# The opening of an encoder block: sums as 128 equal columns, and a new order of loads, rows and scalings

## The chip, the cores and the metric

The kernel runs on one core of one Trainium2 chip. The metric is the time of one execution on the device in microseconds (us), less is better. The core has five engines that run beside each other: PE (TensorE, matrix products), DVE (VectorE), ACT (ScalarE), POOL (GpSimd) and SP (SyncE, which here only issues transfers), and DMA engines that move data between the chip's memory (DRAM), and the on-chip memory (SBUF). PE writes into a second on-chip memory, PSUM.

## The reference

One encoder layer over 1024 positions of width 1024, in float32, conditioned by a vector c:

```python
ada = silu(c) @ w_ada + b_ada                 # 6 x 1024 numbers
shift1, scale1, gate1, shift2, scale2, gate2 = split(ada, 6)
h = rmsnorm(x, g_mix) * (1 + scale1) + shift1
qa, ka, va, qb, kb, vb, ga, gb = split(h @ w_in)
# dilated attention on a, 2-D neighbourhood attention on b, gated merge, w_out
x = x + gate1 * (merged @ w_out)
# second norm with shift2, scale2; w_up, depthwise conv, gelu gate, w_down; final rmsnorm
```

What matters here is the beginning: before the first product of `h` with `w_in` can run, the kernel needs the norm of x (a sum of squares over the 1024 features of every position) and the numbers shift1 and scale1, which come from a product of the vector silu(c) with the 1024 x 2048 first columns of `w_ada`.

## The kernel before, in words

**Layout.** x is kept transposed, features on the 128 partitions, in eight tiles `x[0][k]` of 128 x 512 (the first half of the positions) and eight `x[1][k]` (the second half). A feature product is a sum over k = 0 to 7. Every operand of a product is split in two, a high part rounded to PE's reading format and a low part, the rest, and a product is three: high x high, high x low, low x high. ACT makes the high parts (L57, L229), DVE or POOL the low ones (L61, L231).

**w_ada.** It comes in ten pieces of 512 columns. The first four pieces are shift1 and scale1, cut so that piece q holds what the two feature tiles k = 2q and 2q+1 need: a quarter. A piece is eight rows `wt[q][t]` of 128 x 512. The sum over t and over the partitions is made in two ways. `ada_rows` (L169) lets DVE multiply a row by `cs[:, t]`, a number per partition, and add it to a 128 x 512 sum (`acc`, which lies in PSUM under the name pv); `ada_sums` (L153) lets PE sum over the partitions: four products with a 128 x 128 block of the row as weights and one column moving, which gives one column of four in PSUM (`pada`). Its column is `cs[:, t]` for a row that DVE left alone and `ones` for what DVE added up. `add_sums` (L95) does the same for the squares of x (`pcol`). `piece_bias(q)` (L290) adds b_ada (L293) and makes the scale `am1` (L295). `scaled` (L225) then lets ACT compute h from x with that scale and bias, high part (L229) and the whole once more (L230), and gives DVE's low part (L231) to be called later.

**The opening, in one written order.** Lines 419 to 612 stand in a block in which the program order is the order of every engine's queue: SP, ACT, DVE, POOL and PE each take their instructions one after the other, as they are written. SP's loads are: x[0] (four pairs), the small vectors, piece 0, the first half (k = 0 to 3) of two q/k weight tiles (`half_load(qk_raw, ...)`), the first half of two v weight tiles (`v_raw`), piece 1, the second halves, piece 2, piece 3 row by row, x[1], two more v weight tiles (`v_raw1`) and then pairs of rows of pieces 4 to 9 (`pair_load`). Meanwhile PE runs `warm` (L233), products of ones that are never read. Then come:

- the squares of x[0] (ACT L450, DVE L452), their sum over partitions on PE (L454), the norm's factor r on DVE and ACT (L458 to 461), its spread to all partitions by four transposes (`bcast`, L108, called at L463), and in between PE's sums of rows 0, 1 and 2 of piece 0 and DVE's rows 3 to 7, which PE sums at L474;
- x[0][0] and x[0][1] times the spread factor `pb` (L473); `pbs` is a copy of `pb` in SBUF (L470);
- the loop over q (L476): `piece_bias`, x[0][2] and x[0][3] times `pb` on DVE and x[0][4] to x[0][7] times `pbs` on POOL (both in q = 0), `scaled` for two k, the splits of v weights (`v_split`) and of the second half of q/k weights (`qk_split(1)`, q = 1), DVE's rows of the next piece in portions around the low parts (`steps`), the first rows of the piece after that (L499), and on PE the products of q and k (`qk_products`, L305), the sums of the next piece, and the products of v (`v_parts`, L312).

**After it.** From L518 on the block does v for the second half of the v columns, the norm and modulation of x[1] (`modulate`, L212), and a loop over `v_steps` (L578): in each step PE makes v for one or two blocks of 128 positions (`v_wide`), DVE adds rows of pieces 4 to 9 (`row_pairs`, up to `row_ends[n]`), ACT copies v out of PSUM and SP stores it (`v_out`, L284, through the tile `vs` with two buffers). At L553 and L551 stand the row sums, at L600 and L605 the last sums of each piece. After the block the rest of v (`v_steps[9:]`, L629) and the attention follow.

Of the kernel before, what the change touches and what calls it, by code (L numbers as in the profile page):

```python
# [19 lines left out]
KT = 8  # L20
# [9 lines left out]
def hybrid_encoder(tc, xT, c, w_ada, small, w_in, p1_bias, p23_bias, na_bias, ln2_mult, ident, w_br, w_out,  # L30
# [62 lines left out]
    qkpool = tc.alloc_tile_pool(name="qk", bufs=4)  # L93

# [189 lines left out]
    def v_out(br, st, p, c0=0):  # L284
        vs = work.tile([128, 512], FT, name="vs", bufs=2)[:, :p.shape[-1]]
        act.activation(vs, p, AF.Copy)
        sp.dma_start((va_s, vb_c)[br][st * 128:st * 128 + 128, c0:c0 + p.shape[-1]], vs)
# [17 lines left out]
    def qk_products(ks):  # L305
        for k in ks:
            mhi, mlo = h[0, k]
            for x_, (part, m) in enumerate(((0, mhi), (1, mhi), (0, mlo))):
                for p, w in zip(qk_psum, qk_w):
                    pe.matmul(p, w[part][:, k], m, start=k + x_ == 0, stop=k == KT - 1 and x_ == 2)  # L310
# [108 lines left out]
    with tc.manual_schedule(engines={e.engine for e in (sp, act, dve, pool, pe)}):  # L419
# [26 lines left out]
        warm(35, idle, True)  # L446
# [6 lines left out]
        pcol = ps_n.tile([128, KT], FT, name="pcol")  # L453
# [4 lines left out]
        dve.tensor_scalar(r, pcol[:, :4], 1.0 / D, EPS, OP.mult, OP.add)  # L458
        act.activation(r, r, AF.Sqrt)
        ada_rows(wt[0], acc, range(3, 4), 3, 7)  # L460
# [3 lines left out]
        warm(3, idle, True)  # L464
        ada_sums([(wt[0][1], cs[:, 1:2])], pa, stop=False)
        warm(4, idle, True)
        ada_sums([(wt[0][2], cs[:, 2:3])], pa, stop=False)
        warm(2, idle, True)
        pbs = early.tile([128, 512], FT, name="mt", bufs=3)
        act.activation(pbs, pb, AF.Copy)  # L470
        ada_rows(wt[0], acc, range(4, 8), 3, 7)
        for k in range(2):
            dve.tensor_tensor(x[0][k], x[0][k], pb, OP.mult)  # L473
        ada_sums([(wt[0][7], ones)], pa)  # L474
        warm(5, idle, True)
        for q in range(4):  # L476
            ks = range(2 * q, 2 * q + 2)
            piece_bias(q, pa)
            if q == 0:
                for k in range(2, 4):  # L480
                    dve.tensor_tensor(x[0][k], x[0][k], pb, OP.mult)
                stage = [ps_n.tile([128, 512], FT, name=n) for n in ("pcol", "pbc")]
            low = [scaled(x[0][k], k) for k in ks]
            if q == 0:
                v_split(v_raw, (pool, pool), slice(0, 4), v_w[0])
                for k in range(4, 8):
                    pool.tensor_tensor(x[0][k], x[0][k], pbs, OP.mult)
# [12 lines left out]
            if q == 2:  # L500
                accs = sq_accs()
                square(x[1], accs, range(4), dve)
            if q == 3:
                v_split(v_raw1, (dve, pool), slice(0, KT), v_w[1])
                square(x[1], accs, range(4, 8), dve)
            qk_products(ks)
            if q == 0:
                pa = ada_sums([(wt[1][t], cs[:, t:t + 1]) for t in (6, 7)], stop=False)
                v_parts(0, range(4), ks, (0,))
                ada_sums([(wt[1][5], ones)], pa)  # L510
                v_parts(0, range(4), ks, (1, 2))
                continue
            v_parts(0, (0,), ks, range(3))
# [26 lines left out]
        row_ends = (4, 7, 10, 12, 14, 17, 19, 22, 24)  # L540
# [37 lines left out]
        for n, step in enumerate(v_steps[:9]):  # L578
# [50 lines left out]
    for br, st in v_steps[9:]:  # L629
        v_out(br, st, *v_wide(st))  # L630
# [1279 lines left out]
```

## Time and profile before

| | us |
|---|---|
| median of 3 runs | 1500.61 |
| lowest and highest of them | 1496.16, 1501.8 |
| the profiled execution, its own time | 1498.67 |
| span of its trace | 1496.8 |
| PE busy in the span | 1474.4 |
| DVE, ACT, POOL busy | 939.0, 773.6, 760.6 |

The span is the time from the first to the last instruction in the trace; the time of an execution has 1.87 us more around it. In rows of the trace the first number is the start in us from the span's start, the second the duration (where it says x3, the stretch of three), then engine, line and operation, then what is written <- what is read, with shapes, and in brackets how long the engine stood idle before and what ended that. PEld are PE's weight loads, which run beside its products. A product in plain float32 appears as two records, so a sum of four products is eight. POOL's durations are rough. In tables of stretches the columns are: stretch, its length, busy time and number of records of PE, PEld, DVE, ACT and POOL, the clock granted to PE (1.00 is full), the mean busy share of the DMA engines, and GB/s.

### The profile page before, as it was taken

Reading aid. Unit: us, or ns where it says so; the run is one execution under the profiler, and the core shown is the slowest. Engines: PE = TensorE matmul, PEld = TensorE weight load, DVE = VectorE, ACT = ScalarE, POOL = GpSimd, SP = SyncE. Lnnn points to the kernel's source line nnn. Section 1 sums busy time; section 2 is a strip of 40 time slices with the busy share of each in tenths; the row PEclk is TensorE's granted clock in tenths of the full one; section 3 lists DMA queues with packets and bytes.
Section 4 is the critical chain, followed back from the end, with each engine's and each line's share of the span. In section 5 each row is a group of like instructions: output and inputs, shape, how many; then the busy total and the mean of one; then the engine's idle time right before and its main releaser. Section 6 shows DMA issues by size and latency. Waiting matters only on the chain.

```text
span 1496.8 us, 21659 instructions
## 1 busy us (share of the span) xinstructions
PE 1474.4 (98%) x7664; PEld 1251.9 (84%) x7664; DVE 939.0 (63%) x1763; ACT 773.6 (52%) x1442; POOL 760.6 (51%) x633
## 2 busy tenths in 40 slices
PE   9999999999999999999999999999999999999997
PEld 8888888889798998888888778888888888877887
DVE  7683446465555665556515897666666667886865
ACT  4531666666655666653345464444444447474542
POOL 3031332434234454512268668766666776978811
PEclk9999999999999999999999999999999999999999
DMA  9577332444645555577544313222222233542313
GB/s 371 183 277 268 88 99 68 143 114 129 170 144 145 144 160 166 172 243 260 194 153 143 104 43 141 85 85 85 85 83 84 71 136 116 197 148 64 104 41 113
DMA packets 117301, 210.29 MB, mean 140 GB/s; under 512 B 42788, under 2 KB 55716, under 8 KB 117156
## 3 DMA queue, kind: packets, MB, share of 16 engines
q1 hardware_dynamic: 116632, 208.57, 43.4%
q8 instruction: 60, 0.98, 0.3%
q14 instruction: 49, 0.40, 0.1%
q10 hardware_dynamic: 560, 0.33, 0.1%
HBM read 163.58 MB, written 42.66 MB: 138 GB/s over the span
## 4 chain that ended last, share of the span: by engine, by line
PE 81%; DVE 5%; POOL 5%; DMA 4%; issue 2%; ACT 2%; SPq 0%; DVEq 0%; POOLq 0%; ACTq 0%
PE pj L84 10%; PE pj L86 10%; PE pj L85 10%; PE pj L1308 10%; PE pj L1307 10%; PE pj L1306 10%; PE pj L402 3%; PE O L1013 2%; DMA wraw<-w_down 2%; PE T L1000 1%; PE S L978 1%; POOL wsl L61 1%; PE pv L279 1%; PE pv L281 1%; PE pv L280 1%
## 5 line engine op out<-in xcount | busy, mean ns | idle before, releaser
L61 POOL TENSOR_TENSOR wlo<-wraw,whi 128x512 fp32r<-128x512 f32 (+1 forms) x84 | 106.1, 1284 | 144.8 <-ACT whi L57 129.8
L84 PE MATMUL pj<-h,whi 128*128 128x512 f32 x432 | 178.1, 412 | 0.4 <-DVE kl L374 0.4
L86 PE MATMUL pj<-h,wlo 128*128 128x512 f32 x432 | 169.8, 393 | 0.0
L85 PE MATMUL pj<-h,whi 128*128 128x512 f32 x432 | 169.4, 392 | 0.0
L1306 PE MATMUL pj<-op,wsh 128*128 128x512 f32 x408 | 159.1, 391 | 3.7 <-ACT wsh L57 2.7
L1307 PE MATMUL pj<-op,wsh 128*128 128x512 f32 x408 | 159.1, 390 | 0.9 <-DVE op L1237 0.6
L1308 PE MATMUL pj<-op,wsl 128*128 128x512 f32 x408 | 157.8, 390 | 0.7 <-POOL wsl L61 0.7
L667 DVE TENSOR_TENSOR tl<-T,th 128x512 fp32r<-128x512 f32 (+3 forms) x120 | 77.2, 654 | 101.2 <-ACT th L666 99.9
L717 POOL TENSOR_TENSOR wlo<-wraw,whi 128x512 fp32r<-128x512 f32 x58 | 74.4, 1293 | 126.8 <-ACT whi L716 126.7
L61 POOL TENSOR_TENSOR wsl<-big,wsh 128x512 fp32r<-128x512 f32 (+1 forms) x86 | 111.7, 1320 | 42.5 <-ACT wsh L57 37.6
L659 ACT ACTIVATE P<-P,st 128x256 f32<-128x256 f32 x128 | 64.2, 503 | 93.9 <-DVE st L658 93.9
L1543 DVE SCALAR_TENSOR_TENSOR big<-pj,sm,big 128x512 f32<-128x512 f32 (+2 forms) x183 | 94.9, 563 | 16.5 <-ACT big L1537 15.6
L86 PEld LDWEIGHTS pj<-h,wlo 128*128 128x128 f32 x432 | 81.1, 188 | 18.0
L1306 PEld LDWEIGHTS pj<-op,wsh 128*128 128x128 f32 x408 | 76.6, 188 | 21.9 <-ACT wsh L57 4.0
L1307 PEld LDWEIGHTS pj<-op,wsh 128*128 128x128 f32 x408 | 76.6, 188 | 18.2 <-DVE op L1237 1.2
L1308 PEld LDWEIGHTS pj<-op,wsl 128*128 128x128 f32 x408 | 76.6, 188 | 17.4 <-POOL wsl L61 1.8
L84 PEld LDWEIGHTS pj<-h,whi 128*128 128x128 f32 x432 | 81.5, 189 | 11.5 <-issue 0.8
L1308 PE MATMUL pj<-op,wlo 128*128 128x512 f32 x232 | 90.3, 389 | 0.0
L1307 PE MATMUL pj<-op,whi 128*128 128x512 f32 x232 | 90.3, 389 | 0.0
L1306 PE MATMUL pj<-op,whi 128*128 128x512 f32 x232 | 90.3, 390 | 0.0
L85 PEld LDWEIGHTS pj<-h,whi 128*128 128x128 f32 x432 | 81.7, 189 | 10.1
L61 POOL TENSOR_TENSOR wsl<-wraw,wsh 128x384 fp32r<-128x384 f32 (+1 forms) x46 | 57.3, 1268 | 62.1 <-ACT wsh L57 54.5
(398 smaller groups left out, 4173.6 us busy)
## 6 DMA issues: line engine op xcount, KB each, us to landing
wraw<-w_in SPq DMA_DIRECT2D x32, 512.0 KB
wada<-w_ada SPq DMA_DIRECT2D x31, 512.0 KB
big<-w_up SPq DMA_DIRECT2D x22, 512.0 KB
wraw<-w_up SPq DMA_DIRECT2D x22, 512.0 KB
big<-as SPq DMA_DIRECT2D x22, 512.0 KB
as<-big SPq DMA_DIRECT2D x21, 512.0 KB
gs<-gs SPq DMA_DIRECT2D x32, 256.0 KB
g<-gs SPq DMA_DIRECT2D x16, 512.0 KB
```

What stands on the lines that cost most here:

```text
L61: lo_eng.tensor_tensor(lo[:, i:i + step], raw[:, i:i + step], f(hi)[:, i:i + step], OP.subtract)
L84: pe.matmul(psum, whi[:, k0 + k], mhi, start=k == 0, stop=False)
L85: pe.matmul(psum, whi[:, k0 + k], mlo, start=False, stop=False)
L86: pe.matmul(psum, wlo[:, k0 + k], mhi, start=False, stop=k == n - 1)
L402: pe.matmul(p[:, 256 * r:256 * r + 256], ww[:, k], m[:, r], start=k + x + r == 0, stop=k == KT - 1 and x == 2, skip_group_check=True)
L659: act.activation(pp, pp, AF.Exp, bias=mi, scale=-1.0, accum_out=li)
L667: dve.tensor_tensor(tl[:m, :n], pt[:m, :n], f(th)[:m, :n], OP.subtract)
L717: pool.tensor_tensor(lo[:, i:i + n], raw[:, i:i + n], f(hi)[:, i:i + n], OP.subtract)
L1306: pe.matmul(psum, whi[:, k], bhi, start=j < 4 and k == 0, stop=False, skip_group_check=True)
L1307: pe.matmul(psum, whi[:, k], blo, start=False, stop=False, skip_group_check=True)
L1308: pe.matmul(psum, wlo[:, k], bhi, start=False, stop=k == n - 1, skip_group_check=True)
L1543: dve.scalar_tensor_tensor(y[:, dst], src, wt, y[:, dst], OP.mult, OP.add)
```

## The change

It has six parts.

1. `wide_sums` takes the place of `ada_sums` and `add_sums` in the opening: the moving operand is the column repeated 128 times, so each of the four products gives 128 equal columns, 512 in all. `every` picks column 0 of each 128. It is used for the squares of x[0], for the sums of piece 0, and for the sums of piece 1; later ones stay as they were.
2. Of the 52 dummy products 42 are left: 38 ahead of the sum of squares (35 before) and 4 ahead of the loop.
3. The order around the norm: DVE's row 3 of piece 0 comes ahead of the norm's factor, row 4 between its parts, rows 5 to 7 behind; on PE the sums of rows 0 and 1 come ahead of the transposes.
4. Loads: piece 1 is loaded ahead of the first half of v_raw, and piece 2 ahead of the second halves of the q/k and v weights.
5. In q = 0 POOL scales x[0][2] to x[0][7], DVE none of them; row 3 of piece 1 goes from DVE to PE, between the products of k = 0; one row of piece 3 goes from the end of q = 1 to the first portion of q = 2.
6. In the loop over `v_steps` the stores of v are issued by ACT in place of SP, and a tenth step is in the loop.

```diff
+    def wide_sums(dst, blocks, col, first=False):
+        for m in range(4):
+            cc = slice(m * 128, m * 128 + 128)
+            pe.matmul(dst[:, cc], blocks[:, cc], col.to_broadcast([128, 128]), start=first and m == 0, stop=False,
+                      skip_group_check=True)
+    def every(p):
+        return p.rearrange("p (t c) -> p t c", c=128)[:, :, 0]
...
-    def v_out(br, st, p, c0=0):
+    def v_out(br, st, p, c0=0, queue=sp):
...
-    def qk_products(ks):
+    def qk_products(ks, parts=range(3)):
...
+        wt.append(ada_load(1))
         half_load(v_raw, (8, 9), 0)
-        wt.append(ada_load(1))
+        wt.append(ada_load(2))
         half_load(qk_raw, (0, 4), 1)
         half_load(v_raw, (8, 9), 1)
-        wt.append(ada_load(2))
...
-        warm(35, idle, True)
+        warm(38, idle, True)
...
-        add_sums(pcol, total, True, True)
-        warm(3, idle, True)
-        pa = ada_sums([(wt[0][0], cs[:, 0:1])], stop=False)
+        wide_sums(pcol, total, ones, True)
+        pa = ps_s.tile([128, 512], FT, name="pada", bufs=1)
+        for t in range(2):
+            wide_sums(pa, wt[0][t], cs[:, t:t + 1], t == 0)
         r = wpool.tile([128, KT], FT, name="rs", bufs=2)[:, :4]
-        dve.tensor_scalar(r, pcol[:, :4], 1.0 / D, EPS, OP.mult, OP.add)
+        ada_rows(wt[0], acc, range(3, 4), 3, 7)
+        dve.tensor_scalar(r, every(pcol), 1.0 / D, EPS, OP.mult, OP.add)
         act.activation(r, r, AF.Sqrt)
-        ada_rows(wt[0], acc, range(3, 4), 3, 7)
+        ada_rows(wt[0], acc, range(4, 5), 3, 7)
         dve.reciprocal(r, r)
         qk_split(0, (pool, pool))
         pb = bcast(r, ps_n, "pbc")
-        warm(3, idle, True)
-        ada_sums([(wt[0][1], cs[:, 1:2])], pa, stop=False)
-        warm(4, idle, True)
-        ada_sums([(wt[0][2], cs[:, 2:3])], pa, stop=False)
-        warm(2, idle, True)
+        wide_sums(pa, wt[0][2], cs[:, 2:3])
...
-        ada_rows(wt[0], acc, range(4, 8), 3, 7)
+        ada_rows(wt[0], acc, range(5, 8), 3, 7)
...
-        ada_sums([(wt[0][7], ones)], pa)
-        warm(5, idle, True)
+        wide_sums(pa, wt[0][7], ones)
+        warm(4, idle, True)
...
-            piece_bias(q, pa)
+            piece_bias(q, pa if q > 1 else every(pa))
             if q == 0:
-                for k in range(2, 4):
-                    dve.tensor_tensor(x[0][k], x[0][k], pb, OP.mult)
...
-                for k in range(4, 8):
+                for k in range(2, 8):
                     pool.tensor_tensor(x[0][k], x[0][k], pbs, OP.mult)
...
-            steps = (range(q + 1, 4), range(4, 5), range(5, 7)) if q else (range(0), range(2), range(2, 6))
+            steps = (range(2, 4), range(4, 5), range(5, 7)) if q else ((), (0,), (1, 2, 4, 5))
...
-                ada_rows(wt[q + 2], acc, range(q + 2), 0, 6)
+                ada_rows(wt[q + 2], acc, range(2), 0, 6)
...
-            qk_products(ks)
             if q == 0:
-                pa = ada_sums([(wt[1][t], cs[:, t:t + 1]) for t in (6, 7)], stop=False)
+                qk_products((0,), range(2))
+                pa = ps_s.tile([128, 512], FT, name="pada", bufs=1)
+                wide_sums(pa, wt[1][3], cs[:, 3:4], True)
+                qk_products((0,), range(2, 3))
+                qk_products((1,))
+                for t in (6, 7):
+                    wide_sums(pa, wt[1][t], cs[:, t:t + 1])
                 v_parts(0, range(4), ks, (0,))
-                ada_sums([(wt[1][5], ones)], pa)
+                wide_sums(pa, wt[1][5], ones)
...
-        row_ends = (4, 7, 10, 12, 14, 17, 19, 22, 24)
+        row_ends = (4, 7, 10, 12, 14, 17, 19, 22, 24, 24)
...
-        for n, step in enumerate(v_steps[:9]):
+        for n, step in enumerate(v_steps[:10]):
...
-                    v_out(step[0], st, pp)
+                    v_out(step[0], st, pp, queue=act)
...
-    for br, st in v_steps[9:]:
+    for br, st in v_steps[10:]:
```

More of the change, by code (lines that the diff above doesn't have):

```diff
@@ L282, in v_wide @@
         return ps
-    def v_out(br, st, p, c0=0):
+    def v_out(br, st, p, c0=0, queue=sp):
         vs = work.tile([128, 512], FT, name="vs", bufs=2)[:, :p.shape[-1]]
         act.activation(vs, p, AF.Copy)
-        sp.dma_start((va_s, vb_c)[br][st * 128:st * 128 + 128, c0:c0 + p.shape[-1]], vs)
+        queue.dma_start((va_s, vb_c)[br][st * 128:st * 128 + 128, c0:c0 + p.shape[-1]], vs)
     sig = wpool.tile([128, KT], FT, name="rs", bufs=2)
@@ L303, in qk_split @@
             split(raw[:, 4 * i:4 * i + 4], hi[:, 4 * i:4 * i + 4], lo[:, 4 * i:4 * i + 4], e)
-    def qk_products(ks):
+    def qk_products(ks, parts=range(3)):
         for k in ks:
             mhi, mlo = h[0, k]
-            for x_, (part, m) in enumerate(((0, mhi), (1, mhi), (0, mlo))):
+            for x_ in parts:
+                part, m = ((0, mhi), (1, mhi), (0, mlo))[x_]
                 for p, w in zip(qk_psum, qk_w):
@@ L505, in hybrid_encoder @@
                 square(x[1], accs, range(4, 8), dve)
[L506 removed]
             if q == 0:
[L508 removed]
+                qk_products((0,), range(2))
[5 more added lines that the diff above has]
+                    wide_sums(pa, wt[1][t], cs[:, t:t + 1])
                 v_parts(0, range(4), ks, (0,))
[L510 removed]
+                wide_sums(pa, wt[1][5], ones)
                 v_parts(0, range(4), ks, (1, 2))
                 continue
+            qk_products(ks)
             v_parts(0, (0,), ks, range(3))
```

2 lines of the change are left out of this document (1 added, 1 removed).

## The prediction

> **What bounds the kernel now.** I read the page first, then busy times by stretch, then who waited for whom on TensorE, then the chain of waits of the opening.
>
> ```profile
> span 1496.8 us, 21659 instructions
> ```
>
> ```profile
> 0.00:60.00 60.00, 57.06 (x412) 52.25 (x412) 39.80 (x64) 31.64 (x51) 18.27 (x18) 1.00 0.88 336
> 60.00:200.00 140.00, 139.26 (x723) 116.96 (x723) 82.42 (x157) 58.08 (x129) 35.13 (x31) 1.00 0.55 183
> 200.00:1480.00 1280.00, 1268.89 (x6460) 1074.01 (x6459) 807.37 (x1518) 681.20 (x1256) 703.50 (x580) 1.00 0.41 127
> ```
>
> The columns are the stretch, then busy time on PE, PE's weight loads, DVE, ACT and POOL, the granted clock, the DMA share and GB/s. From 60 us to the end PE is hardly ever idle: 0.74 us are free up to 200 us and 11.1 us (1280 - 1268.89) up to 1480 us. So what the change does after the opening can be worth little, and the opening is worth what it shortens the time until PE runs without a break. In the opening "busy" misleads: PE is filled there with dummy products (L236) and with sums of which four 1-column results are used. The chain shows what really ends last:
>
> ```profile
> 3.40 6.69 DMA kl<-w_ada
> 10.11 9.29 DMA wada<-w_ada
> 19.41 7.80 DMA wada<-w_ada
> 27.32 0.76 DVE pv L174
> ```
>
> That is a line of transfers of w_ada, each let go when an older one has landed, down to 27.32 us, when DVE gets the first rows of the third piece. The DMA engines are full all that time:
>
> ```profile
> 0.00:20.00 20.00, 18.70 (x148) 18.51 (x148) 11.34 (x23) 9.92 (x16) 2.70 (x6) 1.00 0.92 350
> 20.00:40.00 20.00, 18.54 (x118) 15.21 (x117) 17.50 (x27) 10.52 (x17) 12.48 (x10) 1.00 1.04 391
> ```
>
> So there are two limits ahead of 60 us: PE, ACT and DVE in turn up to the first product, and the order of the bytes after it. I mark the progress by piece_bias(q), the small DVE addition at L293 that opens a quarter: T0 to T3 are 19.03, 28.77, 36.60 and 45.09 us now.
>
> **Part 1: up to T0.** These rows (start, duration, what) carry the terms:
>
> ```profile
> 6.57 4.68 DVE L452 TENSOR_TENSOR sq<-sq,mt 128x512 f32<-128x512 f32 x6 [0.26 <-ACT mt L450]
> ...
> 11.30 1.05 PE L98 MATMUL pcol<-ones,sq 128*128 128x1 f32 x8 [0.24 <-DVE sq L452]
> ...
> 12.39 0.16 DVE L458 TENSOR_SCALAR rs<-pcol 128x4 f32<-128x4 f32 x1 [1.14 <-PE pcol L98]
> ...
> 13.12 0.17 DVE L461 RECIPROCAL rs<-rs 128x4 f32<-128x4 f32 x1
> 13.25 2.34 DVE L176 SCALAR_TENSOR_TENSOR pv<-qs,cs,pv 128x512 f32<-128x512 f32 x3
> ...
> 15.70 0.97 PEld L236 LDWEIGHTS pv<-om 128*128 128x128 f32 x8
> 15.73 1.14 PE L236 MATMUL pv<-om 128*128 128x128 f32 x8
> ...
> 16.47 1.29 DVE L473 TENSOR_TENSOR ks<-ks,pbc 128x512 f32<-128x512 f32 x2
> ...
> 17.93 0.97 PEld L160 LDWEIGHTS pada<-ones,qs 128*128 128x128 f32 x8
> ...
> 19.03 0.16 DVE L293 TENSOR_TENSOR ada<-pada,sm 128x4 f32<-128x4 f32 x1 [1.28 <-PE pada L160]
> ...
> 19.42 0.81 ACT L229 ACTIVATE h<-ks,ada,am 128x512 fp32r<-128x512 f32 x1 [2.99 <-DVE am L295]
> ```
>
> A wide sum isn't in this trace. Its nearest row is the dummy product, of the same shape: eight records (four instructions) take 0.97 us of weight loads, as do the eight of a 1-column sum. Its end lies between 1.05 us (the 1-column row) and 1.14 us (the dummy row) after its start; I take 1.14, the row of its own shape. So a sum costs PE the same, and the 17 dummies that stood between the sums (3+3+4+2+5) come off the path, less the 4 that stay and that run while DVE works. At 0.97/8 = 0.12 us a record and two records each, 13 are 3.1 us, of which only what PE now holds up can be won: DVE's 1.28 us of waiting ahead of 19.03, and what its new order gives.
>
> Three more dummies ahead of the chain are 6 x 0.12 = 0.7 us. They end about 0.3 us after DVE's sum of squares (11.25), so pcol is ready at 11.6 + 1.14 = 12.75 instead of 12.35; DVE fills that wait with row 3 (0.78). From there DVE has 0.16 (rstd), row 4 0.78, 0.17 (reciprocal), rows 5 to 7 2.34 and two scalings 1.29, with small gaps: 12.75 + 4.85 = 17.6. PE is ready by then: pcol and two wide sums to 14.5, transposes 0.5, the third sum to 16.0, the last one from 16.3 (when row 7 is done) to 17.45. **T0 is 17.6, 1.4 us earlier.** If the first 38 dummies cost nothing it is 17.3. If the wide sums cost 0.2 more each, PE is last: three of them to 15.1, transposes, the fourth to 16.8, the fifth to 18.1, and so is T0.
>
> **Part 2: T0 to T1.** The bytes come first. Ahead of the third piece's first pair stood 2.10 (x) + 0.13 + 2.10 + 0.52 + 0.52 + 2.10 + 0.52 + 0.52 MB and its own 0.52, 9.1 MB with the small ones; at 350 and 391 GB/s that much is moved at 25.4 us, and it landed at 27.32, 1.9 us later. The second piece's first pair (6.0 MB, moved at 17.4) landed at 10.11 + 9.29 = 19.4, 2.0 us later. With 1.05 MB of weights put behind it, the third piece's pair lands at about 24.7 (estimate: 8.06 MB moved at 22.7, and 2.0). In return the first half of v_raw goes from 5.4 to 7.5 MB and lands at about 23.3.
>
> ```profile
> 21.69 1.20 PE L310 MATMUL pj<-h,whi 128*128 128x512 f32 x4 [0.20 <-DVE h L231]
> ...
> 22.26 1.14 ACT L57 ACTIVATE vwh<-kl 128x512 fp32r<-128x512 f32 x2
> ...
> 24.07 1.98 PEld L160 LDWEIGHTS pada<-cs,wada 128*128 128x128 f32 x16
> ...
> 27.04 0.95 PE L160 MATMUL pada<-ones,wada 128*128 128x1 f32 x8
> ...
> 28.77 0.15 DVE L293 TENSOR_TENSOR ada<-pada,sm 128x4 f32<-128x4 f32 x1
> ```
>
> PE starts the products 1.4 us earlier, at 18.9; the q/k products of two k are twelve, 0.24 to 0.3 us apart (1.20 for four, the last one's own 0.39 included). The new wide sum (row 3 off DVE, 0.97 on PE) fills the wait for DVE's low halves, so the next sums start at 18.9 + 12 x 0.24 + 0.97 = 22.7 against 24.07. From there to the end of the closing sum it is the same work, 27.04 + 0.95 - 24.07 = 3.9: 26.6. DVE is done before: low halves by 21.6, four rows 3.1, two rows of the third piece 1.55, 26.3. The GpSimd scalings of k = 2 and 3 no longer cost DVE its 1.28. **T1 is 26.65, 2.1 us earlier, and PE sets it.** ACT's hi halves of v (23.3 + 1.14 = 24.4) come just ahead of the products that need them (24.6): that cover is 0.2 us thin, and each further us costs one.
>
> **Part 3: T1 to T3.**
>
> ```profile
> 22.96 2.51 POOL L61 TENSOR_TENSOR vwl<-kl,vwh 128x512 fp32r<-128x512 f32 x2 [5.10 <-ACT vwh L57]
> 25.43 2.52 POOL L487 TENSOR_TENSOR ks<-ks,mt 128x512 f32<-128x512 f32 x2
> ```
>
> GpSimd has twelve operations in a row, two for v, six scalings, two for q/k and two for v, at 1.26 (2.51/2): from 23.9 it gives x[2] at 27.7, x[3] at 29.0, the q/k low halves at 36.5 and v's at 39. ACT wants x[2] at 27.1 and waits 0.6; PE has 2.0 us of products of v between, so 0.3 to 0.5 of that reaches it. T2 is then 34.7, 1.9 earlier.
>
> ```profile
> 28.96 0.25 DVE L295 SCALAR_TENSOR_TENSOR am<-ada,sm 128x2 f32<-128x2 f32 x1
> ...
> 35.27 2.53 POOL L61 TENSOR_TENSOR vwl<-kl,vwh 128x512 fp32r<-128x512 f32 x2
> ...
> 36.60 0.15 DVE L293 TENSOR_TENSOR ada<-pada,sm 128x4 f32<-128x4 f32 x1
> 36.79 1.02 DVE L295 SCALAR_TENSOR_TENSOR am<-ada,sm 128x2 f32<-128x2 f32 x1
> ...
> 39.43 0.69 DVE L231 TENSOR_TENSOR h<-pcol,h 128x512 fp32r<-128x512 f32 x1 [0.95 <-ACT pcol L230]
> ...
> 45.09 0.16 DVE L293 TENSOR_TENSOR ada<-pada,sm 128x4 f32<-128x4 f32 x1
> ```
>
> The row of the fourth piece that goes from q = 1 to q = 2 falls into that wait of 0.95, so DVE, which sets T3, loses nothing, and the rest of the quarter takes what it took. The 1.02 is the unknown here: the same instruction took 0.25 at 28.96. It ended at 37.81, when GpSimd's pair of 35.27 ended (37.80), so I read it as a wait for GpSimd. With GpSimd busy from 23.9 to 39 both T1 and T2 can meet it, at 0.25 to 1.26 us each; I take half an operation, 0.6, as nothing sets the phase. At T1 it hides in ACT's wait for x[2]; at T2 it is 0.4 less than now. **At T3, and at 50 us, 2.3 us are left (T3 42.8), and PE then runs on as before.**
>
> The Trainium skill has a rule that speaks against this part: by SBUF — State Buffer, section "Who interferes with whom", a VectorE instruction with two SBUF inputs and a GpSimd instruction that reads SBUF block each other for a whole instruction. The 1.02 us agrees with it; with a whole operation at both places the sum would be 1.2 us in place of 2.3.
>
> **Part 4: v_out on ACT, one step more in the fixed order.** This part lies in the stretch in which PE has 0.74 us free.
>
> ```profile
> 1.15 0.45 ACTq L46 DMA_DIRECT2D idt<-ident  x1
> ```
>
> ```profile
> SPq L287 <- ACT vs L286: 36.9, 10, 10.5
> ```
>
> ```profile
> PE pada L160 <- DVE ada L167: 0.5, 1, 0.5
> PE pv L279 <- ACT vs L286: 0.3, 1, 0.3
> ```
>
> Ten issues go to ACT at 0.45 each, 4.5 us in 140 of which ACT is busy 58; behind them on ACT wait the weight splits of the second branch, which PE covers with 11 us of q/k products. SP loses its 36.9 us of waiting for ACT, so later rows land sooner; DVE's wait for them was not PE's. The whole can be worth from +0.5 (if an issue is ever ahead of a copy that PE needs) to -0.8 (both waits gone); I take 0, since the two sums behind the 0.5 still follow each other.
>
> **Sum.** 1.4 + 0.7 - 0.2 + 0.4 = 2.3 us. The profiled execution took 1498.67 (span 1496.8 and 1.87 around it), so its like would take 1496.4. It lies 1.94 below the median of the three runs shown, 1500.61; against that median I forecast **1498.3 us**.
>
> **Rivals.** (a) **The weights that were moved back are late.** From 23.5 on each us by which v_raw lands later than 23.3 stops PE ahead of its products of v and moves T1 out by one; at 25.8 the gain is gone: 1500.6. For it: a cover of 0.2 us. Against: the two landings worked out in Part 2 lag the byte order by 1.9 and 2.0 us, so they keep to it. (b) **GpSimd becomes the bound, and it is slower than before.** Its pace isn't always 1.26:
>
> ```profile
> 97.94 1.74 POOL L61 TENSOR_TENSOR vwl<-ks,vwh 128x512 fp32r<-128x512 f32 x1
> ```
>
> ```profile
> 42.50 0.31 PEld L320 LDWEIGHTS pv<-vwl,h 128*128 128x128 f32 x2
> ```
>
> There DVE was splitting from SBUF at the same time. At 1.74 the twelve end at 23.9 + 20.9 = 44.8, where PE needed v's low halves at 42.50: 2.3 us later than now, 1502.9. It decides from a mean of (42.5 - 23.9)/12 = 1.55. Against it: DVE's row sums gather in PSUM (pv), and beside them GpSimd kept 1.26. The skill's rule above is the reason it would give. (c) **Something of the opening spreads into the part from 200 us on**, where PE has 11.1 us free: if most of that were won, 1491; if transfers meet the later stages worse, 1508 or more. No row speaks for either.
>
> **How the numbers follow.** Forecast 0.55 (own range 1496.8 to 1500, from T0 17.3, no lock and Part 4's -0.8 to thin covers), (a) 0.17, (b) 0.12, (c) faster 0.06, slower 0.10. The range takes in (a), (b), and the 1496.16 to 1501.8 over which the runs of one kernel scatter: 1493 to 1504.5. A change of 0.5% is 7.5 us, about what a measurement of this kernel can tell from no change: faster by more than that 0.08, within it 0.79, slower 0.13.
>
> **What would show it.** Right: T0 near 17.6 with no wait for pada, the third piece's first row near 24.7, ACT's wait for x[2] under 1 us, PE without a gap from 47 us, and from there each stage 2 to 2.5 us earlier. Wrong: DVE idle ahead of T0; PE waiting for vwh at 24 to 26 us; GpSimd operations of 1.5 us or more between 24 and 40; a lead at 60 us that is gone at 200.

## The result and the profile after

The changed kernel takes **1493.26 us** (median of 16 runs, 1489.85 to 1497.24), the kernel before 1499.72 (16 runs): a ratio of 0.9959 with a 95% interval of [0.9949, 0.9969], some 6.1 us faster (4.6 to 7.6). A second measurement of both, further down, has 4.8 us (3.0 to 6.6). The forecast was 1498.3 against 1500.61, 2.3 us faster; the time lies at the lower edge of the range (1493). The profiled execution took 1489.85. Its span, and its busy times by stretch in the columns of before:

```profile
span 1488.1 us, 21632 instructions
```

```profile
0.00:60.00 60.00, 57.58 (x424) 54.14 (x425) 38.97 (x65) 34.31 (x56) 20.80 (x20) 1.00 0.89 336
60.00:200.00 140.00, 140.00 (x724) 117.78 (x723) 83.16 (x160) 58.47 (x130) 37.75 (x33) 1.00 0.57 185
200.00:1480.00 1280.00, 1273.18 (x6506) 1080.10 (x6504) 809.28 (x1527) 680.83 (x1255) 704.92 (x582) 1.00 0.41 127
```

From 60 to 200 us PE is busy without a break (140.00 of 140.00 us); after that, up to 1480 us, 6.8 us are free where it was 11.1. The chain that ended last shows what the opening hangs on now:

```profile
1.64 5.61 DMA ks<-xT
7.26 8.41 DMA wraw<-w_in
15.72 0.51 issue
16.23 0.59 ACT mt L479
16.88 0.57 issue
17.45 0.68 DVE ks L482
18.23 0.17 DVE am L305
18.43 0.82 ACT h L239
19.29 1.20 PE pj L321 x4
...
25.97 0.89 PE pada L99 x8
26.87 1.91 PE pv L331 x16
```

Before, the chain was a line of w_ada transfers up to 27.32 us. Now the last transfer in it is the first half of the q/k weights, which lands at 15.7 and hands over to ACT; from 19.29 to 60 us the chain is PE. The rows (start, duration, what, idle time before it) that answer to those of before:

```profile
12.81 0.16 DVE L471 TENSOR_SCALAR rs<-pcol 128x4 f32<-128x4 f32 x1 [0.58 <-PE pcol L99]
...
16.84 1.28 DVE L482 TENSOR_TENSOR ks<-ks,pbc 128x512 f32<-128x512 f32 x2 [0.81 <-ACT mt L479]
...
18.04 0.15 DVE L303 TENSOR_TENSOR ada<-pada,sm 128x4 f32<-128x4 f32 x1
...
22.86 1.31 ACT L57 ACTIVATE vwh<-kl 128x512 fp32r<-128x512 f32 x2 [1.54 <-DMA kl<-w_in]
...
25.11 0.76 DVE L184 TENSOR_SCALAR pv<-wada,cs 128x512 f32<-128x512 f32 x1
...
26.90 0.16 DVE L303 TENSOR_TENSOR ada<-pada,sm 128x4 f32<-128x4 f32 x1 [0.24 <-PE pada L99]
...
34.26 0.16 DVE L303 TENSOR_TENSOR ada<-pada,sm 128x4 f32<-128x4 f32 x1 [0.18 <-PE pada L170]
34.46 0.38 DVE L305 SCALAR_TENSOR_TENSOR am<-ada,sm 128x2 f32<-128x2 f32 x1
...
42.11 0.15 DVE L303 TENSOR_TENSOR ada<-pada,sm 128x4 f32<-128x4 f32 x1
```

T0 to T3 are 18.04, 26.90, 34.26 and 42.11, where they were 19.03, 28.77, 36.60 and 45.09: the lead (start of the same instruction before, less its start after) grows from 1.0 to 1.9, 2.3 and 3.0 us. It stays at 3.0 up to 128 us, is 4.2 from 150 to 290, 3.9 at 1270, and jumps to 8.7 by 1380. So there are three places: the opening, one point near 133 us, and a late stretch, 1290 to 1400 us. The profiled pair differs by 8.8 us, the medians by 6.5. That is why two executions do not settle where the time came from.

### The profile page after: what moved, and what is told of

It is laid out like the page before. It is cut to its first block, busy times and chain, and to the rows that moved or that the text cites. A ratio compares the mean times of both kernels' runs of the same rounds, so it can differ in the third digit from the quotient of the medians.

```text
span 1488.1 us, 21632 instructions
## 1 busy us (share of the span) xinstructions
PE 1471.4 (99%) x7652; PEld 1252.4 (84%) x7652; DVE 935.0 (63%) x1760; ACT 773.8 (52%) x1442; POOL 763.5 (51%) x635
## 4 chain that ended last, share of the span: by engine, by line
PE 86%; DVE 5%; DMA 4%; POOL 2%; ACT 1%; issue 1%; SPq 0%; DVEq 0%; POOLq 0%; ACTq 0%
PE pj L1321 11%; PE pj L1320 11%; PE pj L1319 11%; PE pj L84 11%; PE pj L86 10%; PE pj L85 10%; PE pj L413 2%; PE O L1026 2%; PE T L1013 1%; PE S L991 1%; PE pv L289 1%; PE pv L291 1%; PE pv L290 1%; PE O L857 1%; PE O L806 1%
```

## The theory and its rivals

My theory after the two traces: the opening gives 3.0 us and the stores on ACT and the tenth step (part 6 of the change) another 1.2 near 133 us, both carried to the end. The rivals: the later stages absorb a late opening, so that its 3 us are worth less (and the late jump is the real gain); the load order is not what moves T1; the shape of the sums does something that the profiled pair can't show. The experiments undo or add one part each. In what follows "lead" is taken against the first profile of before at a place named; a second profile of before had a lead of -0.1 at 60 us and -1.0 at 160, so differences under 1 us between single profiles carry nothing.

## Experiments on the stores and on the late start

**The stores back on SP.** The changed kernel with part 6 undone:

```diff
-        row_ends = (4, 7, 10, 12, 14, 17, 19, 22, 24, 24)
+        row_ends = (4, 7, 10, 12, 14, 17, 19, 22, 24)
-        for n, step in enumerate(v_steps[:10]):
+        for n, step in enumerate(v_steps[:9]):
-                    v_out(step[0], st, pp, queue=act)
+                    v_out(step[0], st, pp)
-    for br, st in v_steps[10:]:
+    for br, st in v_steps[9:]:
```

> The changed kernel with its part 6 undone: the stores of v are issued by SP again and the fixed order ends after nine steps. In the two profiles at hand the changed kernel leads by 2.98 us from 45 to 130 us and by 4.20 us from 150 to 290 us, so 1.24 us come from the stretch between. Theory (part 6 takes PE's waits for v's PSUM banks and for pada away): the lead stays at 2.9 to 3.1 us from 45 to 250 us, PE waits for ACT's copy L296 and for pada again, and the time is 1.2 us above the changed kernel. Rival (the opening alone did it, rows simply came at a better moment): the lead goes to 4.2 us by 150 us here too, and the time is that of the changed kernel.

Measured: 1494.44 us (median of 12 runs), and against the kernel before on the same chip a ratio of 0.9963 [0.9949, 0.9977]; the results below are written in the same way. The lead is 2.7 at 45 us and 2.9 from 160 to 1300. The step near 133 is gone and PE's waits from 60 to 160 us are back, at 0.6:

```profile
PE pada L170 <- DVE ada L177: 0.4, 1, 0.4
PE pv L289 <- ACT vs L296: 0.2, 1, 0.2
```

The step at 133 us belongs to part 6. The medians can't tell its worth (this kernel is 1.2 us above the 1493.26 of the changed one and 0.3 below its second measurement, 1494.75); the lead says 1.3 (4.2 - 2.9). What happens there is seen by setting this kernel beside the changed one. First the one with the stores on SP:

```profile
122.85 5.29 DVE L566 SCALAR_TENSOR_TENSOR sq<-wada,cs,sq 128x512 f32<-128x512 f32 x6 [10.17 <-DMA wada<-w_ada]
...
130.81 0.15 DVE L177 TENSOR_TENSOR ada<-pada,sm 128x4 f32<-128x4 f32 x1
...
131.12 1.02 PE L170 MATMUL pada<-ones,sq 128*128 128x1 f32 x8 [0.42 <-DVE ada L177]
```

Then the changed kernel:

```profile
123.04 5.36 DVE L566 SCALAR_TENSOR_TENSOR sq<-wada,cs,sq 128x512 f32<-128x512 f32 x6 [10.80 <-DMA wada<-w_ada]
...
131.07 0.15 DVE L177 TENSOR_TENSOR ada<-pada,sm 128x4 f32<-128x4 f32 x1
...
133.25 0.94 PE L170 MATMUL pada<-ones,sq 128*128 128x1 f32 x8
```

DVE is not earlier: the rows of w_ada reach it 0.2 us later with the stores on ACT, and its bias (L177), which must have read `pada` ahead of the next sum, starts 0.26 later. It is PE that comes later to that sum, at 133.25 instead of 131.12. In the order of instructions 33 products stand between this sum and the one before it without part 6, and 48 with it: the tenth step puts 15 products of its own there. They cover DVE's bias, and PE doesn't wait.

**Before, with part 6 alone** (the reverse edits, `queue=act` in the loop over ten steps).

> The kernel before with part 6 alone. Theory: no lead up to 120 us, 1.2 us (0.8 to 1.5) at 200 us, and a time 1 to 2 us below before. Rival (part 6 is worth something only when the opening is earlier): no lead at 200 us and the time of before within 0.1%. Beyond 200 us its instructions stand in the order of before on every engine; if the 4.5 us that the two profiles differ by between 1270 and 1380 us belong to the change, they are missing here; if they are a matter of the single execution, any value from 0 to 5 us can appear.

Measured: 1497.85 (12), 0.9983 [0.9967, 0.9999]. Its profile starts 0.5 us late (T0 19.55) and gains at the same place as the changed kernel: the lead of PE's products is -0.55 at 120 us and +0.69 at 160, and both of PE's waits are gone. All ten profiles of kernels with part 6 show this step against the first profile of before, 1.24 us in each. Of the kernels with the stores and the steps of before, the second profile of before and the one with wide sums alone, both below, lose 0.8 and 0.9 us there against that first profile, so part 6 is worth 1.2 to 2.1 us, as the execution has it. SP waits less for ACT's copies, 21.8 us instead of 36.9:

```profile
SPq L287 <- ACT vs L286: 21.8, 4, 10.5
```

But DVE starts on the rows of w_ada at 127.03, where the first profile of before has 125.51: what SP saved did not bring those rows sooner. Which part of the second wait (PE for ACT's copy, 0.2 to 0.6) the earlier stores removed, and which the order, was not separated.

**A later start.** Twelve more dummies in the first block:

```diff
-        warm(38, idle, True)
+        warm(50, idle, True)
```

> The changed kernel with twelve dummy products more ahead of the sum of squares, 24 records of 0.12 us: pcol is 2.9 us later, and what follows with it. Theory (the path from pcol on is the bound, and the rest of the program moves as one piece): piece_bias(0) at 20.9 us, a lead of 1.2 to 1.5 us at 200 us in place of 4.20, and a time about 2.9 us above the changed kernel. Rival 1 (landings are the bound of the opening, and pcol has slack): less than 1.5 us of the 2.9 is left at 60 us. Rival 2 (the late 4.5 us hang on where the opening ends): the lead after 1380 us falls back by clearly more than 2.9, to below 2.

Measured: 1497.06 (12), 0.9976 [0.9964, 0.9988]. T0 is 20.77 (2.7 later than in the changed kernel), T1 29.63, T2 37.88, T3 45.70. The delay grows from 2.7 us at T0 to 3.6 at T3 (45.70 for 42.11), which the theory did not have. From there it stays: the lead is 0.5 to 0.7 from 160 to 800 us where the changed kernel has 4.2. The medians differ by 3.8 (against 1493.26) or, on the same chip, by 2.6 from the 1494.44 above, whose lead at 160 us is 2.2 more. A delay at the start isn't absorbed later; that rival fell. The late gain comes here as well (+2.8 from 1280 to 1400), so it doesn't hang on when the opening ends.

## Experiments on the opening

**The old order of loads.** Part 4 of the change alone undone:

```diff
-        wt.append(ada_load(1))
         half_load(v_raw, (8, 9), 0)
-        wt.append(ada_load(2))
+        wt.append(ada_load(1))
         half_load(qk_raw, (0, 4), 1)
         half_load(v_raw, (8, 9), 1)
+        wt.append(ada_load(2))
```

> The changed kernel with its part 4 undone: SP loads the weights ahead of pieces 1 and 2 as before. Theory (byte order): piece_bias(0) stays at 18.0, but the third piece's first rows land at about 27 us, where DVE waits for them, and piece_bias(1) comes at 28.3 to 28.8 in place of 26.90; of the changed kernel's lead of 4.2 us at 200 us 2.4 to 3.2 are left, and the median is 1 to 1.8 us above it. Rival (DVE and PE bound the quarter, landings are hidden): piece_bias(1) within 0.5 us of 26.9, the lead 4.0 or more.

Measured: 1496.33 (10), 0.9962 [0.9948, 0.9976]; T0 18.20, T1 29.35, T2 39.26, T3 46.90.

```profile
27.89 0.76 DVE L184 TENSOR_SCALAR pv<-wada,cs 128x512 f32<-128x512 f32 x1 [2.67 <-DMA wada<-w_ada]
28.69 0.76 DVE L186 SCALAR_TENSOR_TENSOR pv<-wada,cs,pv 128x512 f32<-128x512 f32 x1
29.35 0.15 DVE L303 TENSOR_TENSOR ada<-pada,sm 128x4 f32<-128x4 f32 x1
29.54 1.31 DVE L305 SCALAR_TENSOR_TENSOR am<-ada,sm 128x2 f32<-128x2 f32 x1
```

DVE waits 2.67 us for the third piece again, and T1 is 2.45 later: the load order moves T1, as the count of bytes said. I had expected it to keep a lead of 2.4 to 3.2 us at 200 us; it has none (-1.9 at 45 us, -0.6 at 200). Two more things befell that one execution, the 1.31 us of `am` and 3.4 us of half clock at 33 us, and it was the slowest of its ten. What part 4 is worth in time isn't settled: on the same chip this kernel is 2.0 us above the one with all sums wide (1494.29, below), but its ratio lies between the 0.9959 and the 0.9968 of the changed kernel's two measurements. T0 stays early here (18.20), as it does with narrow sums in the new order (18.20, below), and with wide sums alone, below, it doesn't come early (19.66). So the 1 us at T0 comes from the dummies and the order around the norm (parts 2 and 3), which were not tried apart.

**GpSimd's scalings back on DVE** (k = 2 and 3, as before the change):

```diff
             if q == 0:
+                for k in range(2, 4):
+                    dve.tensor_tensor(x[0][k], x[0][k], pb, OP.mult)
...
-                for k in range(2, 8):
+                for k in range(4, 8):
```

> The changed kernel with the scalings of x[0][2] and x[0][3] back on DVE in the first quarter and four on GpSimd. Theory (DVE has room in that quarter): DVE's 1.3 us come ahead of the rows of piece 1, so the low part of k = 0 stays on time, the rows end at about 26.4 instead of 25.1 and, with two rows of piece 2 behind them, piece_bias(1) comes at 27.9 to 28.2 instead of 26.90; the lead at 200 us falls from 4.2 to 2.9 to 3.3. Rival (ACT waits less for x[2], and that pays for it): piece_bias(1) later by a microsecond, but the lead at 200 us 3.9 or more.

Measured: 1493.78 (5), 0.9963 [0.9949, 0.9977]; T0 to T3 17.95, 26.80, 34.22, 42.09, the lead 3.0 at 45 us and 4.2 at 160. My expectation of a later T1 fell. The first row below is of the changed kernel and shows the gap that DVE has there, the two behind it are of this one and show what became of it:

```profile
19.94 0.69 DVE L241 TENSOR_TENSOR h<-pcol,h 128x512 fp32r<-128x512 f32 x1 [1.55 <-ACT pcol L240]
```

```profile
18.22 1.28 DVE L490 TENSOR_TENSOR ks<-ks,pbc 128x512 f32<-128x512 f32 x2
...
19.85 0.69 DVE L241 TENSOR_TENSOR h<-pcol,h 128x512 fp32r<-128x512 f32 x1 [0.36 <-ACT pcol L240]
```

The 1.28 us fit into a wait of 1.55. The move to GpSimd by itself shows no gain in the profile.

**ACT's copy of pbc ahead of the weight splits.** `act.activation(pbs, pb, AF.Copy)` goes ahead of `qk_split(0, ...)`, as the changed kernel's chain runs through a copy that stands behind a split waiting for its weights.

> The changed kernel with ACT's copy of the spread factor (pbs) written ahead of ACT's first split of the q/k weights instead of behind it. In the changed kernel DVE stood idle 0.81 us ahead of the first scaling, put down to that copy, which stood behind a split that waited for a landing. Theory: DVE's first scaling starts at about 16.1 instead of 16.84, piece_bias(0) at 17.5 to 17.7 instead of 18.04, and 0.3 to 0.5 us of that is left at 60 us, if the low parts of the q/k weights on GpSimd (now done at 17.9, then at about 18.7) still come ahead of PE's need of them at 18.9. Rival (the last sum on PE is the bound): piece_bias(0) stays at 18.0.

Measured: 1494.51 (12), 0.9958 [0.9943, 0.9973]. From rstd to T0 the profile needs 4.46 us instead of 5.23, so the wait is real, but this execution began 0.8 us late (rstd at 13.60) and T1 is 26.93, as before the edit. No gain in time can be told.

## Experiments on the shape of the sums

Every execution comes with a mean granted clock. The changed kernel has 0.9962 on average over 16 executions. The kernel before has 0.9949 (35), 0.9934 (25) and 0.9953 (19) on the three chips of the experiments, 0.9945 over all 79; standard errors are 0.0003 to 0.0004, so the three differ by more than their errors, and kernels are best compared on one chip. The profiled pair had 0.998 and 0.997: it doesn't show this, and has it the other way round. (In that profile of before, half clock stands only at the end, from 1489.9 us on; every profile has 4 to 7 us of it there.) So I separated the shape from the order.

**Narrow sums in the places of the wide ones:**

```diff
-            pe.matmul(dst[:, cc], blocks[:, cc], col.to_broadcast([128, 128]), start=first and m == 0, stop=False,
+            pe.matmul(dst[:, m * 128:m * 128 + 1], blocks[:, cc], col, start=first and m == 0, stop=False,
```

> The changed kernel with every wide sum turned back into one of a single moving column, in the same places and the same order. So far: the executions of the kernel before had a mean granted clock of 0.9949 (35 of them), those of the kernel with part 6 alone 0.9946 (12), and those of the four kernels with the new opening 0.9962, 0.9965, 0.9965 and 0.9968; times fall by about 1.1 to 1.2 us for each 0.001. Theory (the wide sums keep TensorE's clock up; the records of a 1-column sum keep PE occupied but hardly load it): the lead over the profile of before stays at 4.0 to 4.4 us at 200 us where no window of half clock falls into the opening, but the mean clock falls to 0.995 and the median is 1 to 2.5 us above that of the changed kernel. Rival (the shape is worth nothing for the clock; the order alone closed PE's gaps): clock 0.996 to 0.997 and the median of the changed kernel within 0.7 us.

Measured: 1496.18 (10), 0.996 [0.9945, 0.9974], mean clock 0.9942. Its profiled execution ran from 17.3 to 27.5 us at half clock, and again from 30.9 to 34.3. The third column from the end is the granted clock; this kernel, then the changed one:

```profile
14.00:18.00 4.00, 3.76 (x31) 3.68 (x32) 3.61 (x7) 1.75 (x3) 2.12 (x2) 0.91 1.04 404
18.00:22.00 4.00, 4.00 (x16) 3.61 (x17) 2.36 (x6) 2.89 (x4) 0.39 (x1) 0.50 1.03 400
22.00:26.00 4.00, 4.00 (x13) 3.42 (x14) 3.86 (x6) 1.26 (x2) 2.41 (x2) 0.50 1.03 409
26.00:30.00 4.00, 4.00 (x30) 3.81 (x28) 0.77 (x2) 0.00 (x0) 4.00 (x5) 0.81 1.04 390
```

```profile
18.00:22.00 4.00, 2.84 (x18) 2.40 (x17) 2.36 (x7) 2.90 (x4) 0.00 (x0) 1.00 1.04 411
22.00:26.00 4.00, 4.00 (x32) 3.78 (x31) 3.82 (x7) 1.26 (x2) 2.43 (x2) 1.00 1.03 410
26.00:30.00 4.00, 4.00 (x29) 3.48 (x29) 3.53 (x7) 2.57 (x4) 4.00 (x5) 1.00 1.03 388
```

From 22 to 26 us PE is called busy 4.00 of 4.00 us in both, but at half clock four q/k products (L321) take 2.05 us (at 23.13) where the changed kernel's take 1.18 (at 21.14). Nor do the rows tell why the clock falls: in the 3.4 us ahead of 17.3 PE is busy for 3.17 us here and for 3.22 in the changed kernel, and from 18 to 22 us it is the changed kernel whose PE stands idle, for 1.16 us, and it keeps its full clock. T0 is still 18.20, but T1 is 30.80 and T3 48.21. The Trainium skill, TensorE: Matmul & The Clock Gate, section "What's actually happening", has the gate at half or at full by how busy PE was in a free-running window of about 3.4 us; the lengths here, 10.2 and 3.4 us, are three such windows and one.

**Wide sums alone in the kernel before** (those of the norm and of the first two pieces, in the old order, with the old dummies between them):

```diff
-        add_sums(pcol, total, True, True)
+        wide_sums(pcol, total, ones, True)
...
-        ada_sums([(wt[0][1], cs[:, 1:2])], pa, stop=False)
+        wide_sums(pa, wt[0][1], cs[:, 1:2])
...
```

> The kernel before with part 1 alone: the sums of the squares, of piece 0 and of piece 1 are wide, all dummy products, orders, loads, scalings and stores as before. Theory: a wide sum takes PE as long as a narrow one (0.97 us of weight loads for four products), so the lead over the profile of before stays within 0.3 us of zero; but the mean clock rises from 0.995 to 0.996 or more and the median falls 0.7 to 2 us below before. Rival (the clock follows from PE's idle time between 20 and 42 us, which this kernel keeps): clock 0.995 and no gain. Rival 2 (wide sums are slower on PE): a lead below -0.5 us.

Measured: 1498.68 (12), 0.9984 [0.9971, 0.9996], mean clock 0.9967. Its profile has no lead anywhere up to 1300 us (-0.6 at 60 us, -1.9 at 1260): T0 is 19.66, T3 45.70, and PE's waits from 60 to 160 us are 1.6. And yet the median is 3.2 us below that of before on the same chip. That profiled execution, at 1501.07, was one of the slower of the twelve.

**The remaining sums of the opening wide too** (those of q = 1 and 2, and of the norm of the second branch), in the changed kernel.

> The changed kernel with the remaining 1-column sums ahead of 60 us made wide as well: those of pieces 2 and 3, which PE makes in pairs of about 2 us at 32 and 40 us, and the two for the squares of x[1]. Theory of the clock: the mean granted clock rises above that of the changed kernel's opening (0.9962 to 0.9968), to 0.997 or more, and the median comes 0.3 to 1.5 us below it; the lead at 200 us stays 4.0 to 4.4. Rival: clock and median as in the changed kernel.

Measured: 1494.29 (6), 0.9952 [0.9933, 0.997], mean clock 0.9968, lead 2.8 at 45 us and 3.9 at 160. Not to be told from the changed kernel.

**Both: all wide, and the copy ahead.**

> The changed kernel with the copy of the spread factor ahead of ACT's first split and with all sums ahead of 60 us wide. Theory: from the norm's first step on DVE (L471) to piece_bias(0) it takes 4.5 us in place of 5.23, and with the clock of the wide kernels (0.9965 or more) the median is 0.5 to 1.5 us below that of the changed kernel in the same call. Rival: the quarter that follows is bound by landings and the closing sum, so that the 0.7 us are gone at piece_bias(1), and the medians are within 0.5 us.

Measured: 1493.05 (11), 0.9961 [0.9948, 0.9973], mean clock 0.9970. T0 to T3 are 17.27, 26.44, 34.45, 42.18.

```profile
12.79 0.16 DVE L471 TENSOR_SCALAR rs<-pcol 128x4 f32<-128x4 f32 x1 [0.51 <-PE pcol L99]
...
17.27 0.16 DVE L303 TENSOR_TENSOR ada<-pada,sm 128x4 f32<-128x4 f32 x1
...
24.96 0.76 DVE L184 TENSOR_SCALAR pv<-wada,cs 128x512 f32<-128x512 f32 x1 [0.65 <-DMA wada<-w_ada]
```

Rstd comes when it did in the changed kernel (12.81), and T0 0.77 sooner, so here the copy is worth its 0.8. Then DVE runs into the landing of the third piece, 0.65 of waiting where the changed kernel had none, 0.46 is left at T1, and nothing at T2. The wait on the third piece is shown; that bytes alone bound the opening now is not, since `am` took 0.79 us behind T1 here and 0.23 in the changed kernel.

**Both kernels again.** The changed kernel and the one before, unaltered.

> The changed kernel itself, as a second execution with a profile and as the measure for the other kernels of this call. Expected: piece_bias(0) to (3) within 0.5 us of 18.04, 26.90, 34.26 and 42.11, a lead of 4.0 to 4.4 us at 200 us, a mean clock of 0.996 to 0.997. Open: the stretch from 1290 to 1400 us, where PE waited 0.4 us in its first profile and 3.7 in that of before, and 0.5 to 3.1 in eight others, all with the same order of instructions. If that is a matter of the execution, it may well be 1 to 3 here.

> The kernel before itself, for a second profile. If the clock is what its opening pays for, a window of half clock can show ahead of 45 us, as it did in two of three profiles with narrow sums there (at 29 us and at 17 us); without one, the lead over its first profile stays within 0.8 us of zero up to 1300 us. In the stretch from 1290 to 1400 us PE's waits are 2 to 4 us if they belong to this kernel, anything from 0.5 if they belong to the execution.

Measured: the changed kernel 1494.75 (9 runs, 1489.84 to 1495.88), 0.9968 [0.9956, 0.998], mean clock 0.9962, lead 3.2 at 45 us and 4.4 at 200; before 1498.29 in the one execution with a profile, against a median of 1499.08 (19) on that chip. The ratio is 4.8 us (3.0 to 6.6) of 1499. The second profile of before has T0 to T3 at 19.10, 28.71, 36.66 and 45.15, and PE's waits from 60 to 160 us are larger than in the first:

```profile
PE pada L160 <- DVE ada L167: 1.0, 1, 1.0
PE pv L279 <- ACT vs L286: 0.6, 1, 0.6
```

## What the clock is worth

One of the chips had all four combinations; the numbers are mean granted clocks, with the number of executions:

| | narrow sums | wide sums |
|---|---|---|
| old order | 0.9934 (before, 25) | 0.9967 (wide sums alone, 12) |
| new order | 0.9942 (narrow in the places of the wide, 10) | 0.9968 (all wide, 6), 0.9961 (old loads, 10) |

The shape goes with the clock and the order shows no effect: wide is 0.002 to 0.003 higher in both rows, with standard errors of 0.0003 to 0.0005, while the two narrow kernels differ by 0.0008. On the two other chips the kernels with wide sums have 0.9962 to 0.9970, those with narrow ones 0.9946 to 0.9953. The smallest of these gaps, 0.0010, is that of the changed kernel itself (0.9962 of 9) and before (0.9953 of 19). In the profiles, half clock fell ahead of 45 us in two of the four with narrow sums (part 6 alone, and narrow) and in one of the ten with wide ones (the old loads).

Over the 79 executions of before a line through clock and time falls by 1.05 us for each 0.001 (0.7 to 1.2 on single chips). By it the 0.0017 between 0.9945 and 0.9962 are about 1.8 us, and gaps of 0.0010 to 0.0033 are 1.0 to 3.5 us. The shape alone was worth 2.4 us (0.6 to 4.3) by its own ratio. Against that stands the narrow kernel, whose ratio (0.996) is no worse than that of the changed one: it was 1.9 us above the all-wide variant on the same chip, less than these intervals can tell. That wide sums raise the clock is shown; their price is known to about 2 us either way; that they do it by keeping PE's array busier is my reading and was not tried.

The sum is then 3.0 (opening) + 1.2 (part 6) + 1.8 (clock) = 6.0 us, against 6.1 (4.6 to 7.6) and 4.8 (3.0 to 6.6) measured. That it comes so near is partly luck: part 6 can be 2.1, the clock 1.0 to 3.5, and the late stretch, which rival (c) below takes up, isn't in it.

## Why the prediction was partly right

The forecast had 2.3 of the 6.1 us, all from the opening. The time is 0.3 us inside the stated range and outside the 1496.8 to 1500 that the forecast gave itself; the lower end of the range was there for the scatter of single runs, so that the time lies in it is luck.

**Part 1.** T0 was forecast at 17.6 and is 18.04. PE was ready, as forecast, and the wide sums cost it what narrow ones did (0.97 of weight loads for eight records). What was missed is the `[0.81 <-ACT mt L479]` above: DVE's scaling starts after ACT's copy, which stood behind a split that waited for the first q/k weights. Of the forecast 1.4 us, 1.0 came.

**Part 2.** T1 is 26.90, forecast at 26.65, and PE sets it, as forecast. The third piece's first row was used at 25.11, without a wait (its landing was forecast at about 24.7); v_raw was used by ACT at 22.86, as soon as it had landed (forecast 23.3). (In the kernel with the copy ahead and all sums wide, where DVE waits for that row, it is used at 24.96.) The count of bytes held to 0.5 us, though one of its two supports was miscounted: 6.0 MB at 350 GB/s are moved at 17.1 us and not 17.4, so that landing lagged by 2.3 us. Rival (a), late weights, did not come. My reason for GpSimd's scalings was wrong: they gave nothing, since DVE had a gap for them.

**Part 3.** T2 is 34.26, forecast at 34.7, and T3 42.11, forecast at 42.8. At 27.43 ACT waits for `am`, not for x[2], which GpSimd had at 27.3, so the 0.3 to 0.5 us put for that wait did not come; and `am` took 0.23 and 0.38, where 0.6 was put. Rival (b), GpSimd as the bound, did not come: its pairs take 2.52 to 2.56 as before. **The opening gave 3.0 us for the 2.3 of the forecast.** The 0.6 for `am` was taken since "nothing sets the phase". Over all runs and places the instruction does spread, from 0.16 to 1.31 us, but behind T2 it took 0.90 to 1.03 in the four profiles with the old opening and 0.23 to 0.41 in eight of the ten with the new one (0.16 and 1.29 in the two whose T2 was latest): at that place it goes with the order.

**Part 4 failed.** The step was "I take 0, since the two sums behind the 0.5 still follow each other". The tenth step puts 15 more products between them, which I had not counted out, and the wait is gone. The other half of the step, that SP's shorter wait makes later rows land sooner, was wrong as well, as they landed no sooner. And PE's weight loads show more than the 0.8 that I took as the bound from PE's matmuls; in the kernel before:

```profile
PEld pada L160 <- issue: 0.9, 1, 0.9
PEld pv L279 <- ACT vs L286: 0.7, 1, 0.7
```

In the changed kernel neither row is there. Of 0.8 us of waits by the matmuls, or 1.6 by the weight loads, PE gained 1.24.

**The clock was no term of the sum.** "So a sum costs PE the same" is right for its rows and wrong for the program: what the shape does to the clock of later work was not asked, with the granted clock beside every stretch. That is the second failing step; it is worth about 1.8 us by the line above, and no more exactly known than to 2 us.

**Rival (c)** stays open. The late stretch holds 4.8 of the 8.8 us between the first two profiles. PE's waits from 1290 to 1400 us are 3.7 and 3.3 in the two profiles of before, and in those of the changed kernel 0.4 and 2.0; the other variants lie from 0.5 to 3.1, with the same order of instructions in all. The changed kernel's own two profiles differ by 1.6 us there, so much of it is scatter. Not all of it is: the four profiles with the old opening have waits of 2.7 to 3.7 us there (3.2 on average), the ten with the new one 0.4 to 3.1 (1.7). Between 1280 and 1400 us the ten gain 0.3 to 4.8 us on the first profile of before (2.8 on average) and the three others with the old opening 0.8 to 1.3. Between 290 and 1280 us, in turn, profiles with the new opening lose 0 to 1.7 us (and the one with half clock at 804 us loses 3.6). So about 1.5 us more seem to come with the new opening on average. Why is not known, and it is a term that neither the prediction nor the sum above has. One piece can be seen. DVE's addition from SBUF among GpSimd's operations, before:

```profile
1354.31 3.60 DVE L1273 TENSOR_TENSOR big<-wraw,big 128x384 f32<-128x384 f32 x1 [4.07 <-POOL wsl L61]
...
1356.20 1.29 POOL L1381 TENSOR_TENSOR big<-big,wc 128x512 f32<-128x512 f32 x1
```

And after:

```profile
1348.43 2.32 POOL L61 TENSOR_TENSOR wsl<-wraw,wsh 128x384 fp32r<-128x384 f32 x2
1348.52 1.35 DVE L1286 TENSOR_TENSOR big<-wraw,big 128x384 f32<-128x384 f32 x1 [3.20 <-POOL wsl L61]
```

The one took 3.60 us and ended 0.4 after a run of GpSimd operations, the other 1.35. That the phase between the two engines decides it is argued, not tried; whether the change shifts the odds of this piece isn't known.

## What to carry to other kernels

Price an operation on PE twice: by its own rows, and by the granted clock of the program, over many executions; with two kinds of sum of equal duration the program's clock differed here by 0.001 to 0.003, by the line above 1 to 3 us of 1500. Where one engine's step is moved ahead, count out what then stands between each producer and its consumer: 15 products put there hid a wait that looked fixed. Where one profile of each kernel differs by more than the medians do, count a stretch as won only when it is won in every profile with the change.

## What the runs showed of the hardware

A stretch of half clock came with PE's rows called busy throughout, 10.2 us long at 17.3 us in the narrow kernel. But for the one at the end of each profile, the stretches are 3.4, 6.8 or 10.2 us long. Three cost about half their length to all of it (1.5 us of lead for 3.4 us at 1462 us with part 6 alone, 3.0 for 6.8 at 1457 in the changed kernel's second profile, 3.3 for 3.4 at 804 with the old loads), and the one at 391 us in the changed kernel's first profile cost nothing: the lead is 4.3 on both sides. A VectorE operation on two columns (`am`), both inputs in SBUF, took 0.16 to 1.31 us beside GpSimd. The Trainium skill, SBUF — State Buffer, section "Who interferes with whom", has such a VectorE instruction blocked for a whole GpSimd instruction (1.26 us here); the 1.31 agrees, and the 3.60 above is longer than one such instruction explains.
